# A new written-out order for a streamed sum of reciprocals: 30 row transfers, a ring of 41 rows, 72 sums of halves

## The chip, the core and the metric

The kernel runs on one core of a Trainium2 chip. The metric is the device time of one execution in microseconds (us). The core has five engines with queues of their own: TensorE (PE in the profile), VectorE (DVE), ScalarE (ACT), GpSimd (POOL) and SyncE (SP), which here only issues transfers. The profile shows a matmul's weight load as PEld.

## The reference

```python
x = abs(randn(32, 512, 1024)) as float32, + 1e-6
out = np.sum(1.0 / x, axis=-1)        # float32, shape (32, 512)
```

That is 16,384 sums of 1,024 reciprocals. The input is 67.11 MB and is read once; the output is 0.07 MB.

## The kernel before

**Tiling.** The 16,384 sums are laid out as 128 partitions by 128 "rows": row r of a partition is one vector of 1,024 numbers (4 KB), so a row over all partitions is 512 KB. Rows are loaded into `ring`, a buffer of R = 40 rows in SBUF; row r lies in place r mod R. A second SBUF buffer, `prod`, has NP = 22 slots of 512 numbers, and `ps` is the eight PSUM banks, 512 numbers each. `sums` collects one number per row.

**The arithmetic of a row.** A row is cut into halves a and b of 512 numbers. Because 1/a + 1/b = (a + b) / (ab), one reciprocal serves two elements. The reciprocal itself is exp(-ln(S ab)), with a scale S that the last step takes out again. So a row needs four steps, and the list below names each by a letter and the row number:

- the product ab, into a slot of `prod`: on POOL (`P`, line 199), or on DVE (line 220) with both halves from the ring (`W`), or with half b first copied into a PSUM bank by TensorE (`C`, line 209: a matmul with the identity) and then multiplied from there (`V`)
- `L`, the logarithm on ACT, in place in the slot (line 242)
- `E`, the exponential on ACT (line 251): in place, or, if the list gives `@bank`, into a PSUM bank
- `R`, the product with the numerator and the sum over the row, on DVE (line 267). There are two kinds. If TensorE has formed a + b in a PSUM bank (`S`, line 232: two matmuls with the identity that accumulate), `R` is 512 wide: slot times bank. If not, `R` is 1,024 wide: the row in the ring times the bank that holds the exponential, which is read twice.

One float32 matmul of the source appears as two MATMUL records in the profile, so an `S` is four records and a `C` two.

`D` loads rows (line 187). A number behind `+` takes several rows in one instruction (`L26+2` is rows 26 and 27). Numbers behind `@` give the slot for `L` and the bank for `C`, `S` and `E`. Rows 126 and 127 are loaded and worked in two halves each, called 126 to 129 in the list, with 256 numbers where others have 512.

**What sets the order.** There is no loop over rows: the string PLAN is the whole program, one token for each step, and each engine works through its own tokens in the order in which they stand. Before, rows 0 to about 80 follow a pattern of four rows: two with 1,024-wide `R` and an exponential in PSUM, two with `S`; ACT works mostly on pairs; about every eighth row is a `C` and `V`. From row 80 on the list is irregular. `note` (line 135) records which spaces each step reads and writes and drops waits that follow from others. The loads wait until the rows that stood in their places of the ring are done. The sums of rows 0 to 113 are written out in six transfers (line 289) when all of these are complete, the last 14 at the very end (line 291).

The tail of the list decides the end. Before, it reads:

```
R121 ... W124 ... R122 ... W125 S125@1 ... R123 P126 ... P127 ... S127@0 R124 ... P128 ... S128@2 ...
P129 R125 ... S129@3 ... R126 ... R127 ... R128 R129
```

Of the kernel before, what the change touches and what calls it, by code (L numbers as in the profile page):

```python
# [11 lines left out]
def kernel(  # L12
# [5 lines left out]
    nc = tc.nc  # L18
# [2 lines left out]
    D = 1024  # L21
    H = D // 2
    F = 128
    R = 40
    NP = 22
    LAST = F - 2  # L26
    DONE = 114
    S = float(2**17)

    PLAN = """
        D2 D10 D14 D14 P0+2 C3@3 S2@0 V3 P2 L0+2@0 C11@3 S3@1 E0+2@6 P4+2 V11 L2+2@2 R0 S6@2
        E2+2 R1 P6+2 L4+2@4 R2 R3 E4+2@6 S7@0 P8+2 L6+2@8 R4 S10@1 E6+2 R5 P10 L8+2@10 R6 R7  # L40
        S11@2 E8+2@6 L10+2@6 R8 E10+2 R9 D11 R10 R11 P12+2 C19@3 S14@0 V19 P14+2 L12+2@12
        S15@1 E12+2@6 S18@2 R12 P16+2 L14+2@16 R13 E14+2 R14 P18 L16+2@18 R15 S19@0 E16+2@6
        P20+2 L18+2@14 R16 S22@1 E18+2 R17 D9 P22+2 L20+2@20 R18 R19 E20+2@6 S23@2 P24+2
        L22+2@0 R20 E22+2 R21 L24+2@2 R22 R23 E24+2@6 P26 C27@3 R24 S26@0 P28+2 V27 R25 D7
        L26+2@4 C35@3 E26+2 S27@1 P30+2 V35 L28+2@8 R26 S30@2 R27 E28+2@6 P32+2 L30+2@10 R28
        S31@0 E30+2 R29 P34 L32+2@12 S34@1 R30 R31 E32+2@6 P36+2 S35@0 L34+2@6 R32 E34+2 R33
        D7 P38+2 S38@2 L36+2@16 R34 R35 E36+2@6 S39@1 P40+2 L38+2@18 R36 C43@3 E38+2 R37 D6
        S42@0 P42 L40+2@14 V43 R38 E40+2@6 P44+2 R39 S43@2 L42+2@20 R40 E42+2 S46@1 R41 D3
        P46+2 L44+2@0 R42 R43 E44+2@6 S47@0 P48+2 L46+2@2 R44 S50@2 E46+2 R45 P50 L48+2@4
        R46 C51@3 R47 E48+2@6 S51@1 P52+2 V51 R48 D6 L50+2@8 C59@3 E50+2 R49 P54+2 S54@0  # L50
        L52+2@10 V59 R50 E52+2@6 R51 S55@2 P56+2 L54+2@12 R52 E54+2 S58@1 R53 D5 P58
        L56+2@16 R54 R55 E56+2@6 S59@0 P60+2 L58+2@6 R56 S62@2 E58+2 R57 D4 P62+2 L60+2@14
        R58 R59 E60+2@6 S63@1 P64+2 L62+2@18 R60 S66@0 E62+2 R61 D4 P66 L64+2@20 R62 C67@3
        R63 E64+2@6 P68+2 S67@2 V67 R64 L66+2@0 S70@1 R65 D4 E66+2 P70+2 L68+2@2 R66 R67
        S71@0 E68+2@6 P72+2 L70+2@4 R68 D3 E70+2 R69 D2 C75@3 P74 L72+2@10 S74@2 R70 V75
        P76+2 E72+2@6 R71 S75@1 L74+2@8 R72 D2 E74+2 R73 D2 P80 S78@0 L76+2@12 R74 P81
        L80@16 R75 S79@2 E76+2@6 P78+2 L81@17 R76 D2 S81@1 E80@5 E81 R80 L78+2@6 W82 E78+2
        R81 R77 D1 D1 D1 D1 D1 P88 C85@6 S85@1 R78 P83 L88@18 V85 E88@7 R79 P84 S84@0
        L82+2@14 R88 E82+2@5 P86+2 L84+2@19 R82 D1 E84+2 R83 D1 D1 D1 C90@7 P91 L86+2@0
        S91@2 R85 P93 V90 E86+2@5 R84 P92 S90@1 L90+2@2 R87 L93@21 W89 L92@10 R86 D1 D1 D1  # L60
        D1 E93@7 P94 S97@0 E92@6 R93 E90+2 P97 S94@3 L89@11 R92 E89@7 P95 L97@8 R91 S95@4
        E97 R90 L94+2@4 W96 R97 P101 C99@6 L96@9 R89 E94+2 S100@0 P98 V99 E96@5 L101@12 R95
        P100 S99@1 L98@13 R96 E101@7 L99+2@16 R101 E98@6 P104 C103@5 R94 E99+2 S105@2 R98
        P102 L104@18 V103 E104@7 W105 L102+2@6 R100 P107+2 C106@6 L105@14 R104 E102+2@4
        S108@0 V106 E105 R102 L106+3@19 P109 S107@3 R103 P110 E106+3 R105 S106@4 R99 P111+2
        L109+2@0 R107 S112@1 R108 E109+2@6 R106 L111+2@10 P114 R109 S111@0 E111+2 R110 P113
        L114@15 R111 C115@7 P116 L113@2 R112 E114@6 V115 E113@5 S117@0 P117 R114 L116@3
        L115@8 P118 E116@7 R113 S118@1 E115@6 P119 L117+2@12 R116 E117+2 R115 P120 S120@2
        L119@9 R117 P121 L120@4 S121@3 R118 E119@7 E120 R119 P122 L121@5 S122@0 E121 R120
        P123 L122@18 R121 E122 W124 L123@6 R122 L124@7 W125 S125@1 E123@7 E124@6 R123 P126  # L70
        L125@14 P127 L126@16 S127@0 R124 E125 P128 L127@17 S128@2 E126@7 P129 R125 E127
        S129@3 L128@19 R126 L129@20 E128 R127 E129 R128 R129
    """.split()

    Ln = mybir.ActivationFunctionType.Ln
# [26 lines left out]
    make_identity(nc, ident)  # L102

    def parse(tok):
        body, _, b = tok[1:].partition("@")
        r, _, n = body.partition("+")
        return tok[0], int(r), int(n or 1), int(b) if b else None

    ops = [parse(tok) for tok in PLAN]

    pslot = {r + j: b + j for op, r, n, b in ops if op == "L" for j in range(n)}

    def place(r):
        if r < LAST:
# [9 lines left out]
    left = set(range(DONE))  # L124
    bank, copied, halves, summed = {}, {}, set(), set()

    history = {}
    begun = {}
    count = {}

    def note(engine, inst, reads=(), writes=()):
        inst = inst.ins
        known = dict(begun.get(engine, {}))
        before = {}
        for spaces, writing in ((reads, False), (writes, True)):
            for space in spaces:  # L140
                for other in history.get(space, ()):
                    if writing or other[3]:
                        before[other[0].name] = other
        needed = sorted(before.values(), key=lambda o: -o[4])
        for other in needed:
            o_inst, o_engine, o_tick, _, _, o_known = other
            if o_engine == engine:
                continue
            if o_tick <= known.get(o_engine, 0):
                tc.declare_no_dep(inst, o_inst, reason="implied by other waits")  # L150
                continue
            for e, t in o_known.items():
                known[e] = max(known.get(e, 0), t)
            known[o_engine] = max(known.get(o_engine, 0), o_tick)
        count[engine] = count.get(engine, 0) + 1
        begun[engine] = known
        entry = (engine, count[engine])
        if engine == "SP":
            entry = (f"load {count[engine]}", 1)
        for spaces, writing in ((reads, False), (writes, True)):  # L160
            for space in spaces:
                history.setdefault(space, []).append(
                    (inst, *entry, writing, sum(count.values()), known)
                )

    def rows(r, n, h=None):
        spaces = []
# [7 lines left out]
    def slots(r, n):  # L175
        return [("slot", pslot[q]) for q in range(r, r + n)]

    with tc.manual_schedule():
        for op, r, n, b in ops:
            p = pslot.get(r)  # L180
            if op == "D":
                n, r = r, loaded
# [45 lines left out]
            elif op == "S":  # L228
                bank[r] = b
                halves.add(r)  # L230
                for h in range(2):
                    inst = nc.tensor.matmul(  # L232
                        ps[:, b, : place(r)[2]],
                        lhsT=ident,
                        rhs=xs(r, h),
                        start=h == 0,
                        stop=h == 1,
                    )
                    note("PE", inst, rows(r, 1, h), [("bank", b)])
            elif op == "L":  # L240
                pg = prod[:, p : p + n, : place(r)[2]]
                inst = nc.scalar.activation(out=pg, in_=pg, func=Ln, scale=S)  # L242
# [1 line left out]
            elif op == "E":  # L244
# [5 lines left out]
                        bank[r + j] = b + j  # L250
                inst = nc.scalar.activation(out=rc, in_=pg, func=Exp, scale=-1.0)  # L251
                if b is None:
                    note("ACT", inst, writes=slots(r, n))
                else:
                    banks = [("bank", b + j) for j in range(n)]
                    note("ACT", inst, slots(r, n), banks)
            elif op == "R":
                q, at, w = place(r)
                other = ps[:, bank[r], :w]
                if r in halves:  # L260
                    row = prod[:, p, :w]
                else:
                    row = ring[:, q % R, at : at + 2 * w]
                    row = row.rearrange("p (h e) -> p h e", h=2)
                    other = other.unsqueeze(1).to_broadcast([P, 2, w])
                total = sums[:, q : q + 1]
                inst = nc.vector.tensor_tensor_reduce(  # L267
                    out=row,
                    in0=row,
                    in1=other,  # L270
                    scale=S,
                    scalar=total if q in summed else 0.0,
                    op0=mult,
                    op1=add,
                    accum_out=total,
                )
                summed.add(q)
                note(
                    "DVE",
                    inst,  # L280
                    [("bank", bank[r])],
                    slots(r, 1) if r in halves else rows(r, 1),
                )

                left.discard(r)
                if not left:
                    for c in range(0, DONE, DONE // 6):
                        part = slice(c, min(c + DONE // 6, DONE))
                        nc.sync.dma_start(out=out_v[:, part], in_=sums[:, part])
                    left.add(-1)  # L290
        nc.sync.dma_start(out=out_v[:, DONE:], in_=sums[:, DONE:])


# [28 lines left out]
```

## Time and profile before

| what | us |
|---|---|
| median of 3 executions (168.05 to 168.22) | 168.14 |
| span of the profiled execution, first to last instruction | 166.31 |
| median less span: what lies around the span | 1.83 |
| first product starts (row 0) | 5.66 |
| first work of TensorE and DVE (row 3) | 17.81, 19.89 |
| last DVE step ends, last transfer is issued | 164.0, 164.06 |
| busy: PE / DVE / ACT / POOL | 132.5 / 128.3 / 132.3 / 128.2 |
| share of 16 DMA engines in row transfers | 95.6% of the span |

The profile gives the span of its execution and no other time for it; the median is of other executions of the same program. The profile's times run from the start of the span. A busy PE is modelled, since matmuls are pipelined: the time from one record's start to the next is the better measure of its rate. The same holds for DVE and ACT, where an instruction overlaps the next by some 0.08 us. "Idle before" of a group of instructions is the time in which the engine stood still ahead of them, with what ended it.

### The profile page before, as it was taken

To read this page: it belongs to the slowest core of one execution; us is meant where nothing else is said; L and a number is where in the kernel's file an instruction comes from. 1 tells how busy PE (TensorE), PEld (TensorE's weight loads), DVE (VectorE), ACT (ScalarE), POOL (GpSimd) and SP (SyncE) were. 2 spreads that over 40 slices of the span, in tenths; PEclk is the share of its full clock that TensorE was granted. 3 is DMA by queue.
4 is the path that set the end of the run, shared out by engine and by line. 5 is a ranking of instruction groups with operands and counts; after the bars stand their busy time and mean duration, and the time that the engine had idled before them with its cause. 6 is when DMAs were issued, how large, how long until landed. Compare 5 with 4: busy or idle time off the path is not lost.

```text
span 166.3 us, 1348 instructions
## 1 busy us (share of the span) xinstructions
PE 132.5 (80%) x292; PEld 55.2 (33%) x292; DVE 128.3 (77%) x282; ACT 132.3 (80%) x157; POOL 128.2 (77%) x81
## 2 busy tenths in 40 slices
PE   0000799978855999999999999988699979989982
PEld 0000333333312444444343433324234424433351
DVE  0000119885787699898998898989899999999994
ACT  3040073949995899999799999996999999999992
POOL 1500795069995999999999999948977869999860
PEclk9999999999996999999999999999999999999999
DMA  5999999999998989999999999999999999999940
GB/s 189 536 394 394 441 441 441 441 441 441 441 441 349 509 368 446 430 417 438 441 434 434 406 426 446 429 424 424 414 437 437 414 410 428 410 409 410 400 139 4
DMA packets 5768, 67.26 MB, mean 404 GB/s; under 512 B 1536, under 2 KB 1536, under 8 KB 3200
## 3 DMA queue, kind: packets, MB, share of 16 engines
q1 hardware_dynamic: 5760, 67.18, 95.6%
q8 instruction: 2, 0.03, 0.1%
q14 instruction: 6, 0.05, 0.1%
HBM read 67.11 MB, written 0.07 MB: 404 GB/s over the span
## 4 chain that ended last, share of the span: by engine, by line
DMA 57%; PE 18%; ACT 8%; DVE 6%; POOL 6%; issue 3%; SPq 1%; ACTq 0%; POOLq 0%; DVEq 0%
DMA ring<-in_x_dram 57%; PE ps L232 15%; POOL prod L199 6%; ACT prod L242 4%; PE ps L209 3%; ACT ps L251 2%; DVE ring L267 2%; DVE prod L267 2%; ACT prod L251 2%; DVE prod L220 1%; SPq L187 1%; DVE sums L267 0%; ACTq L242 0%; POOLq L199 0%; DVEq L317 0%
## 5 line engine op out<-in xcount | busy, mean ns | idle before, releaser
L199 POOL TENSOR_TENSOR prod<-ring 128x1024 f32<-128x1024 f32 (+2 forms) x75 | 127.5, 1727 | 33.5 <-DMA ring<-in_x_dram 27.1
L232 PE MATMUL ps<-ring,ident 128*128 128x512 f32 (+1 forms) x260 | 116.9, 596 | 5.2 <-DVE sums L267 4.5
L242 ACT ACTIVATE prod<-prod 128x1024 f32<-128x1024 f32 (+2 forms) x78 | 68.5, 892 | 24.9 <-DVE prod L220 14.3
L267 DVE CUSTOM_DVE_ANT_1 ring<-ring,ps 128x1024 f32<-128x1024 f32 (+1 forms) x65 | 76.4, 1208 | 8.9 <-ACT ps L251 8.7
L232 PEld LDWEIGHTS ps<-ring,ident 128*128 128x128 f32 x260 | 49.2, 193 | 71.7 <-issue 51.6
L267 DVE CUSTOM_DVE_ANT_0 prod<-prod,ps 128x512 f32<-128x512 f32 (+1 forms) x63 | 40.9, 677 | 0.4 <-PE ps L232 0.4
L209 PE MATMUL ps<-ring,ident 128*128 128x512 f32 x32 | 19.3, 689 | 25.7 <-DMA ring<-in_x_dram 24.0
L251 ACT ACTIVATE ps<-prod 128x1024 f32<-128x1024 f32 (+2 forms) x41 | 34.1, 838 | 4.5 <-DVE sums L267 3.7
L251 ACT ACTIVATE prod<-prod 128x1024 f32<-128x1024 f32 (+3 forms) x37 | 34.4, 931 | 0.9
L220 DVE TENSOR_TENSOR prod<-ring,ps 128x512 f32<-128x512 f32 x16 | 10.9, 684 | 26.3 <-PE ps L209 26.3
L209 PEld LDWEIGHTS ps<-ring,ident 128*128 128x128 f32 x32 | 6.0, 213 | 36.0 <-issue 21.4
L267 DVE DVE_READ_ACCUMULATOR2_ANT sums<- 128x1 f32 x130 | 10.7, 82 | 0.0
L220 DVE TENSOR_TENSOR prod<-ring 128x512 f32<-128x512 f32 x6 | 4.1, 688 | 0.1
L84 ACT ACT_TABLE_LOAD x1 | 1.3, 1283 | 0.7 <-PEq L306 0.7
L267 DVE CUSTOM_DVE_ANT_0 prod<-prod,ps,sums 128x256 f32<-128x256 f32 x2 | 0.9, 475 | 0.0
masks.py:197 POOL MEMSET ident<- 128x128 f32 x1 | 0.2, 204 | 0.3 <-POOLq L306 0.3
masks.py:199 POOL TENSOR_SCALAR_AFFINE_SELECT ident<-ident 128x128 f32<-128x128 f32 x1 | 0.3, 292 | 0.1
L306 POOL MEMSET const-float32-0.0<- 128x1 f32 x1 | 0.1, 98 | 0.2 <-issue 0.2
L306 POOL MEMSET const-bfloat16-1.0<- 128x1 bf16 x1 | 0.1, 101 | 0.0
L306 POOL MEMSET const-uint8-127<- 128x1 uint8 x1 | 0.1, 101 | 0.0
L306 POOL MEMSET const-float32-1.0<- 128x1 f32 x1 | 0.1, 98 | 0.0
## 6 DMA issues: line engine op xcount, KB each, us to landing
ring<-in_x_dram SPq DMA_DIRECT2D x2, 7168.0 KB, 41.2
ring<-in_x_dram SPq DMA_DIRECT2D x2, 3584.0 KB, 29.3
ring<-in_x_dram SPq DMA_DIRECT2D x2, 3072.0 KB, 31.9
ring<-in_x_dram SPq DMA_DIRECT2D x3, 2048.0 KB, 34.0
ring<-in_x_dram SPq DMA_DIRECT2D x1, 5632.0 KB, 30.3
ring<-in_x_dram SPq DMA_DIRECT2D x5, 1024.0 KB, 31.8
ring<-in_x_dram SPq DMA_DIRECT2D x1, 5120.0 KB, 16.5
ring<-in_x_dram SPq DMA_DIRECT2D x1, 4608.0 KB, 30.7
```

The source lines that it names most:

```text
L84: nc.scalar.add_instruction(mybir.InstLoadActFuncSet(name=nc.get_next_instruction_name(), act_func_set_id=act_sets.index("natural_log_exp_ ...
L187: inst = nc.sync.dma_start(out=ring[:, a : a + m, at : at + 2 * w], in_=x_v[:, q : q + m, at : at + 2 * w],)
L199: inst = nc.gpsimd.tensor_tensor(out=prod[:, p : p + m, :w], in0=ring[:, a : a + m, at : at + w], in1=ring[:, a : a + m, at + w : at + 2 * w],
L209: inst = nc.tensor.matmul(ps[:, b, : place(r)[2]], lhsT=ident, rhs=xs(r, 1), start=True, stop=True,)
L220: inst = nc.vector.tensor_tensor(out=prod[:, p, :w], in0=xs(r, 0), in1=in1, op=mult)
L232: inst = nc.tensor.matmul(ps[:, b, : place(r)[2]], lhsT=ident, rhs=xs(r, h), start=h == 0, stop=h == 1,)
L242: inst = nc.scalar.activation(out=pg, in_=pg, func=Ln, scale=S)
L251: inst = nc.scalar.activation(out=rc, in_=pg, func=Exp, scale=-1.0)
L267: inst = nc.vector.tensor_tensor_reduce(out=row, in0=row, in1=other, scale=S, scalar=total if q in summed else 0.0, op0=mult, op1=add, acc ...
L306: nc = _bacc.Bacc("TRN2", target_bir_lowering=False, num_devices=1)
```

## The change

PLAN is replaced as a whole; R goes from 40 to 41 and NP from 22 to 20 (the two buffers together keep their size). Counted over the lists:

| | before | after |
|---|---|---|
| loads `D` (rows in each) | 33 (2, 10, 14, 14, 11, 9, 7, 7, 6, 3, 6, 5, 4, 4, 4, 3, 2 x4, then single rows) | 30 (14, 15, 12, 9, 9, 8, 8, 7, 6, 6, 5, 4, 4, 3, 2 x4, then single rows) |
| sums of halves `S` | 65 | 72 |
| copies `C` | 16 | 20 |
| DVE products `V` + `W` | 16 + 6 | 20 + 13 |
| POOL instructions (products) | 75 (108) | 77 (97) |
| ACT instructions `L` + `E` | 156 | 192 |
| `E` of one row, of two | 27, 50 | 91, 15 |

The rows with `W` are now 1, 7, 17, 14, 34, 40, 55, 62, 67, 82, 93, 124 and 125; before they were 82, 89, 96, 105, 124 and 125. `L` takes up to four rows in one instruction, and `L` and `E` of different rows alternate.

Two things are new in the code. A token can end in `!`: such an `E` (29 of them) waits, besides its own data, for the sum `S` of its rows, so that the `R` behind it has one engine less to wait for. And `note` now also drops a wait of an engine on itself where another wait implies it, and counts `sums` as a space that `R` writes. Two further letters, `A` and `Z`, can be parsed but do not occur in the list.

```diff
-    R = 40
-    NP = 22
+    R = 41
+    NP = 20
...
     PLAN = """
-        D2 D10 D14 D14 P0+2 C3@3 S2@0 V3 P2 L0+2@0 C11@3 S3@1 E0+2@6 P4+2 V11 L2+2@2 R0 S6@2
...
+        D14 D15 D12 W1 C3@0 W7 C5@1 V3 P0 C12@2 V5 P4 L0+2@0 S1@0 V12 E0@1 P6 L3+2@3 R0 S2@7
+        P10+2 L5+2@5 E3 S3@1 E1! L7@2 R1 P8+2 E5@2 S9@3 R3 E4@0 E6 R5 E7@1 P2 S6@4 L8+4@7 R7 P13
+        R4 S8@2 D9 L2@0 L12@11 R6 E2! L13@1 S11@0 R2 E10@1 E8+2! R10 S13@4 E11+2 R9 R8 E13 R11
+        S12@3 R13 W17 C18@0 W14 L17@0 C19@1 R12 P15+2 L14@1 V18 C26@2 E14@3 V19 L18@4 S15@0 R14
+        E18 P22 L15+2@2 V26 S18@1 E17@7 P20+2 E15! R17 E16@2 S21@3 L26@9 R15 R16 D9 P23+2
+        L19+2@5 S24@0 R18 E19+2@4 L21+2@7 R19 P27+2 S23@1 E21! R20 E22@2 S26@4 R21 P25 L27@10
+        L28@11 E26+3 S27@3 L23+3@12 R26 W34 C29@7 R27 P30 E24! C32@6 V29 E23! E25@3 R24 S30@4
...
+        R115 P120 L119@2 R116 E117 E119@2 P121 S121@4 R117 L120@0 E118! R119 P122 E120@0 S122@1
+        L121@1 R118 P123 L122@2 R120 E121! S123@2 E122 W124 L123@0 R121 L124@3 W125 E123 S125@0
+        R122 E124@3 P126 L125@4 R123 P127 L126@1 R124 S126@1 E125 P128 E126 S128@2 P129 L127@2
+        R125 L128@0 E127@3 R126 S129@4 L129@3 R127 E128 E129 R128 R129
...
-    def note(engine, inst, reads=(), writes=()):
+    def note(engine, inst, reads=(), writes=(), after=()):
...
+        for other in after:
+            before[other[0].name] = other
+            tc.add_manual_dep(inst, other[0].name, sync, reason="sums are ready")
...
-            if o_engine == engine:
-                continue
             if o_tick <= known.get(o_engine, 0):
                 tc.declare_no_dep(inst, o_inst, reason="implied by other waits")
                 continue
+            if o_engine == engine:
+                continue
...
-                    note("PE", inst, rows(r, 1, h), [("bank", b)])
+                    sum_of[r] = note("PE", inst, rows(r, 1, h), [("bank", b)])
...
-                    note("ACT", inst, writes=slots(r, n))
+                    after = [sum_of[r + j] for j in range(n) if held]
+                    note("ACT", inst, writes=slots(r, n), after=after)
...
-                    slots(r, 1) if r in halves else rows(r, 1),
+                    (slots(r, 1) if r in halves else rows(r, 1)) + [("sum", q)],
```

More of the change, by code (lines that the diff above doesn't have):

```diff
@@ L38 @@
     PLAN = """
-        D2 D10 D14 D14 P0+2 C3@3 S2@0 V3 P2 L0+2@0 C11@3 S3@1 E0+2@6 P4+2 V11 L2+2@2 R0 S6@2
[L40 to L72, printed above, removed]
+        D14 D15 D12 W1 C3@0 W7 C5@1 V3 P0 C12@2 V5 P4 L0+2@0 S1@0 V12 E0@1 P6 L3+2@3 R0 S2@7
+        P10+2 L5+2@5 E3 S3@1 E1! L7@2 R1 P8+2 E5@2 S9@3 R3 E4@0 E6 R5 E7@1 P2 S6@4 L8+4@7 R7 P13
@@ new lines @@
+        R4 S8@2 D9 L2@0 L12@11 R6 E2! L13@1 S11@0 R2 E10@1 E8+2! R10 S13@4 E11+2 R9 R8 E13 R11
[3 more added lines that the diff above has]
+        L28@11 E26+3 S27@3 L23+3@12 R26 W34 C29@7 R27 P30 E24! C32@6 V29 E23! E25@3 R24 S30@4
+        P31 L29+2@4 R25 P33 E29@0 V32 S31@5 E30 R23 P37 L31+2@6 R22 D8 S35@1 E32@3 P35+2 R29
@@ new lines @@
+        E31! L37@4 S28@2 R32 E37 P38 L33+4@0 R31 S37@0 R28 P39 L38@7 E33@2 W40 S38@3 E34@5 R33
+        D8 L39@16 P41+2 E35! R34 C47@7 L40@17 E38! S40@2 R35 R37 P46 L41+2@18 R38 S41@0 E36@1
+        R30 P49 E39+3 R36 P44+2 S43@3 V47 E42@4 L49@1 R40 L47@2 R41 S39@2 D7 E47 R42 P48 S47@0
+        P43 L48@0 R39 E48+2 L43+4@8 S49@1 W55 R47 P50+2 C53@2 E43! R49 E44+2@4 R43 C52@0 V53
+        E46@1 S48@3 P58 V52 R45 L50+4@12 P54 S51@0 R48 R46 P56+2 L54@1 E51 S55@3 R44 D6 E50@2
+        E54@1 R50 E52@7 S53@4 E53 L55+4@3 R52 D6 S57@2 P64 R51 R53 E58@7 P59+2 R54 E55! S59@0
@@ new lines @@
+        E56@4 E57! R55 R58 S60@1 P61 L60@19 L59@18 R56 D5 E60 P63 S65@3 E59! R57 L64@1 R59 P65
+        L63@0 S66@0 E63+2@4 P66 L65@6 R63 L66@7 W62 E65+2! W67 C71@2 L61+2@2 R64 P72+2 S67@4
+        L67@0 V71 E61@5 R66 E62@6 S70@2 R61 D4 P68 E67 R62 D4 P74 L68@1 S71@0 E68@5 R65 P70
+        L72+3@10 R60 S73@3 R67 P69 L70+2@8 R68 D3 S72@1 E73 L69@7 R73 P78 E70! E71+2 R70 C80@7
+        P75+2 E74@2 S81@3 R71 E69@4 V80 R69 D2 D2 P79 L75+2@4 S77@0 R72 E76@4 P77 R74 D2 E75@1
+        S80@5 P81 R75 L77+4@0 R76 D2 D1 P85 C84@1 L81@4 E77! C87@2 V84 P83 E78+2@6 R77 S83@4 V87
@@ new lines @@
+        E80! P86 L84@7 R78 D1 L83@8 S86@0 E84@1 W82 E83! R84 L82@0 S85@6 E81! R83 E82@2 R81
+        L85+2@5 R82 P88+2 C91@1 E85+2! S89@4 V91 R85 L91@4 R86 P90 L87+2@9 S92@6 R80 E91@0 P92
+        E87+2@1 R91 S90@3 L89+2@11 W93 R87 E89+2 P95+2 C94@5 L92+2@0 R88 S94@0 E93@1 V94 E92!
+        P97+2 R93 S96@2 L94+3@2 R89 R92 E94! S97@1 R79 D1 D1 D1 D1 D1 D1 D1 D1 D1 D1 L97@5 P99
+        E95@4 E96! R94 S100@5 P100 L98+2@6 R95 E97! P101 R96 S98@0 L100@8 R97 E98+3 P102 R90
+        C104@1 P103 L101@0 R100 E101@2 R98 S99@3 P105 L102+2@1 V104 R101 L104@3 P106 S103@0 E103
@@ new lines @@
+        R99 E102@1 P107+2 L105+2@4 R102 C109@7 E104+2@5 R103 S109@4 V109 E106@3 P111 R104
+        L107+2@18 S110@7 L109@6 P110 R106 E108@5 R105 P112+2 S113@0 L110+2@7 E107@1 R108 E109+2!
+        S112@2 R107 L112+2@0 P114+2 R109 E111@3 S115@6 E112+2 R110 R111 L114@2 P116 C117@1
+        L115@3 R113 E114@7 P118 S118@3 V117 L116@4 R112 E115! E116@0 P119 R114 S117@1 L117+2@5
+        R115 P120 L119@2 R116 E117 E119@2 P121 S121@4 R117 L120@0 E118! R119 P122 E120@0 S122@1
+        L121@1 R118 P123 L122@2 R120 E121! S123@2 E122 W124 L123@0 R121 L124@3 W125 E123 S125@0
@@ L104, in parse @@
     def parse(tok):
-        body, _, b = tok[1:].partition("@")
+        body, _, b = tok[1:].rstrip("!").partition("@")
         r, _, n = body.partition("+")
-        return tok[0], int(r), int(n or 1), int(b) if b else None
+        return tok[0], int(r), int(n or 1), int(b) if b else None, tok[-1] == "!"
     ops = [parse(tok) for tok in PLAN]
-    pslot = {r + j: b + j for op, r, n, b in ops if op == "L" for j in range(n)}
+    pslot = {r + j: b + j for op, r, n, b, _ in ops if op == "L" for j in range(n)}
     def place(r):
@@ L132 @@
     begun = {}
+    sum_of = {}
+    sync = mybir.DependencyInfo(
+        mybir.DependencyClass.Sync, mybir.DependencyReason.DATA
+    )
     count = {}
-    def note(engine, inst, reads=(), writes=()):
+    def note(engine, inst, reads=(), writes=(), after=()):
         inst = inst.ins
@@ L159, in note @@
             entry = (f"load {count[engine]}", 1)
+        last = None
         for spaces, writing in ((reads, False), (writes, True)):
             for space in spaces:
-                history.setdefault(space, []).append(
-                    (inst, *entry, writing, sum(count.values()), known)
-                )
+                last = (inst, *entry, writing, sum(count.values()), known)
+                history.setdefault(space, []).append(last)
+        return last
     def rows(r, n, h=None):
@@ L178 @@
     with tc.manual_schedule():
-        for op, r, n, b in ops:
+        for op, r, n, b, held in ops:
             p = pslot.get(r)
@@ L256 @@
                     note("ACT", inst, slots(r, n), banks)
+            elif op == "A":
+                q, at, w = place(r)
+                row = ring[:, q % R, at : at + 2 * w]
+                inst = nc.scalar.activation(out=row, in_=row, func=Ln)
+                note("ACT", inst, writes=rows(r, 1))
+            elif op == "Z":
+                q, at, w = place(r)
+                row = ring[:, q % R, at : at + 2 * w]
+                inst = nc.scalar.activation(
+                    out=row,
+                    in_=row,
+                    func=Exp,
+                    scale=-1.0,
+                    accum_out=sums[:, q : q + 1],
+                )
+                summed.add(q)
+                note("ACT", inst, writes=rows(r, 1) + [("sum", q)])
+                left.discard(r)
             elif op == "R":
@@ L281 @@
                     [("bank", bank[r])],
-                    slots(r, 1) if r in halves else rows(r, 1),
+                    (slots(r, 1) if r in halves else rows(r, 1)) + [("sum", q)],
                 )
                 left.discard(r)
[L286 to L290, printed above, removed]
+            if not left:
+                for c in range(0, DONE, DONE // 6):
+                    part = slice(c, min(c + DONE // 6, DONE))
+                    nc.sync.dma_start(out=out_v[:, part], in_=sums[:, part])
+                left.add(-1)
         nc.sync.dma_start(out=out_v[:, DONE:], in_=sums[:, DONE:])
```

## The prediction

> **What bounds the kernel now.** I read the page first, then stretches of the span, then the costs of single instructions, then the order of time at the start, around the products that DVE makes, and at the end.
>
> The page, with its slices and two of its DMA issues:
>
> ```profile
> span 166.3 us, 1348 instructions
> PE 132.5 (80%) x292; PEld 55.2 (33%) x292; DVE 128.3 (77%) x282; ACT 132.3 (80%) x157; POOL 128.2 (77%) x81
> ...
> DMA  5999999999998989999999999999999999999940
> GB/s 189 536 394 394 441 441 441 441 441 441 441 441 349 509 368 446 430 417 438 441 434 434 406 426 446 429 424 424 414 437 437 414 410 428 410 409 410 400 139 4
> ...
> q1 hardware_dynamic: 5760, 67.18, 95.6%
> ...
> ring<-in_x_dram SPq DMA_DIRECT2D x1, 5632.0 KB, 30.3
> ...
> ring<-in_x_dram SPq DMA_DIRECT2D x9, 512.0 KB, 13.8
> ```
>
> The DMA engines are full from the second slice to the 38th: the loads are the bound, and the engines follow. The 11 rows of 5632 KB move in some 13 us but land 30.3 us after their issue, so the queue never ran dry.
>
> Three stretches (busy time and count of each engine, TensorE's clock, DMA share, GB/s):
>
> ```profile
> 17.70:34.60 16.90, 15.55 (x28) 6.16 (x28) 10.34 (x21) 10.05 (x10) 9.44 (x5) 1.00 1.00 434
> 51.60:65.50 13.90, 13.89 (x29) 6.18 (x30) 11.29 (x23) 11.30 (x12) 13.81 (x7) 0.90 0.99 425
> 145.00:157.40 12.40, 11.88 (x27) 4.50 (x25) 12.30 (x28) 12.17 (x20) 12.28 (x10) 1.00 1.02 408
> ```
>
> Rows of 524 KB at 441 GB/s (slices with 14-row transfers) take 1.19 us, at 408 GB/s (single-row transfers, 145 to 157.4) 1.285 us: a transfer costs 0.1 us beyond its bytes.
>
> TensorE's first records:
>
> ```profile
> 17.81 2.04 PE L209 MATMUL ps<-ring,ident 128*128 128x512 f32 x2 [17.81 <-DMA ring<-in_x_dram]
> 19.65 3.62 PE L232 MATMUL ps<-ring,ident 128*128 128x512 f32 x4
> 23.06 1.36 PE L209 MATMUL ps<-ring,ident 128*128 128x512 f32 x2
> 24.26 1.02 PE L232 MATMUL ps<-ring,ident 128*128 128x512 f32 x2
> ```
>
> The chain of waits has 28 later records in 12.02 us, 0.43 us each; here the first eight take 6.45 us instead of 3.44. TensorE starts slow and loses 3.0 us.
>
> The products on DVE, by form, and one beside its neighbour on POOL:
>
> ```profile
> L220 DVE TENSOR_TENSOR prod<-ring,ps 128x512 f32<-128x512 f32 x16 | 10.9, 684 | 26.3 <-PE ps L209 26.3
> L220 DVE TENSOR_TENSOR prod<-ring 128x512 f32<-128x512 f32 x6 | 4.1, 688 | 0.1
> ...
> 128.03 0.69 DVE L220 TENSOR_TENSOR prod<-ring 128x512 f32<-128x512 f32 x1
> 128.71 1.28 POOL L199 TENSOR_TENSOR prod<-ring 128x512 f32<-128x512 f32 x1 [1.13 <-DMA ring<-in_x_dram]
> ```
>
> The sixteen `V` (one half from PSUM) run beside POOL's products, 53.72 within 51.69 to 55.29 for one. The six `W` (both halves from the ring) stand at 111.51, 122.79, 128.03, 136.22, 157.37 and 158.69, and all fall into gaps of POOL; none overlaps a POOL product by more than 0.13 us. What happens when they meet is not in this trace.
>
> The end, on DVE and SP:
>
> ```profile
> 158.69 0.69 DVE L220 TENSOR_TENSOR prod<-ring 128x512 f32<-128x512 f32 x1
> ...
> 163.54 0.47 DVE L267 CUSTOM_DVE_ANT_0 prod<-prod,ps,sums 128x256 f32<-128x256 f32 x1
> 163.95 0.08 DVE L267 DVE_READ_ACCUMULATOR2_ANT sums<- 128x1 f32 x1
> 164.06 0.33 SPq L291 DMA_DIRECT2D out_dram<-sums  x1
> ```
>
> W125 starts 0.02 us after row 125 has landed (158.67 in the trace's landing records), and DVE works without a gap to 164.03: the end is that landing plus 5.34 us of DVE, plus 2.28 us of output. Span 166.31; the median lies 1.83 us above it, and I add that to every span below.
>
> **The change part by part.**
>
> *Loads.* Three transfers fewer: 3 x 0.1 = 0.3 us earlier at the end, so row 125 lands at 158.37. Do the loads still have their places free in time? Counting the work of TensorE and DVE ahead of each release, the tightest (rows 41 to 49, behind S8) is free near 36 and due at the DMA engines at 52.4, 16 us of lead; before, the shortest lead was 15 (issued at 35.1, first packet at 50.7). SP has nothing else queued behind these. Hidden; if it were not, each us late would be one us of time.
>
> *Start.* The first landing is 14 rows instead of 2. Rows 0 to 11 were there at 17.7; two rows more and a transfer less give 20.05. The work of rows 0 and 1 done by 10.2 moves behind it.
>
> *TensorE.* Records: 69 `S` x 4 + 20 `C` x 2 = 316 of 0.43 us, and 12 half-wide of 0.21: 138.2 us (before: 280 and 12, 122.9). From 20.05, with 3.0 us of slow start: 161.25 if it never waits. The last sum, S129, is needed where R129 starts, near 163.2. So TensorE has 2.0 us of room in 143; before it had about 18. Its work is also cut to the landings: from that of row 121 (153.2) on, 9.4 us are left, to 162.6, which leaves 0.6.
>
> *DVE.* Start to start, 1.14 for a 1,024-wide `R`, 0.61 for a 512-wide one, 0.605 for a product: before 64, 63 and 22 of them, 126.2 us with three small ones; after 57, 70 and 33, 129.1. From 20.05 that ends at 149.2: 14 us to spare, most of it spent waiting for `S`.
>
> *ACT.* Start to start 0.52 for one row, 0.96 for a pair, 1.07 where the exponential follows its own logarithm. Before: 46 singles, 100 pairs at a mean of 1.02, 2 triples, 8 half-wide: 131.8. After: 134 x 0.52 + 38 x 0.96 + 6 triples x 1.41 + 6 quads x 1.85 (estimates on the same slope) + 8 x 0.31 = 128.3. Room of 14 us; splitting pairs costs 0.04 us a row, and alternating gains 0.11 a pair. An `E` with `!` blocks the `L` and `E` behind it until TensorE has the sum; `R` needed that sum anyway. Price between -1.1 us of DVE (22 waits fewer at 0.05) and some us of ACT within its room; on the path I take 0.
>
> *POOL.* 97 products for 108: 115 us for 127. Room.
>
> *The tail.* From W125: 0.62 + 3 x 0.61 (R122, R123, R125) + 1.14 (R124) + 0.36 (R126) + 0.61 (R127) + 0.40 + 0.49 = 5.42, against 5.34. With the landing: 164.03 - 0.3 + 0.08 = 163.81, span 166.1, time 167.9. That is the sum if nothing new waits.
>
> *The thirteen `W`.* Seven stand from W17 to W67, and in the list most stand at a landing ahead of POOL's next product: W17 and W14 ahead of P15+2, W34 ahead of P30, W55 ahead of P50+2, W67 ahead of P72+2. That works only if DVE is there when the rows land. For the first I walk it. TensorE does 3 `C` and 8 `S` up to S13: 3 x 0.86 + 8 x 1.72 + 3.0 = 19.3, so 39.4. R13 needs S13 and runs 39.6 to 40.2. Then comes W17, but rows 14 to 28 land at 38.2 and POOL has P15+2 from then to 40.6, and P22, P20+2, P23+2, P27+2, P25 behind it without a gap. Without the slow start, DVE would have been waiting at 37.2. So they meet. If one blocks the other, W17 starts at 40.6; S15 needs the bank that V18 frees, and V18 stands behind W17, W14 and R12. DVE first both times: V18 ends at 43.5, when TensorE is due at S15 (43.7), cost 0. One POOL product (1.24) between the two: 1.1 us of TensorE. POOL first each time: 3.5. I take 1.1, the case between. W34 comes the same way (TensorE ends S26, ahead of it, at 54.0; its row lands at 52.6): half a single product, 0.6. W40, W55 and W67 sit before pairs of 2.33; an even chance of half of one, 0.6 each. From there on DVE's lateness passes to TensorE through the banks: by counts, releases such as R59 for S66 or R65 for S73 come only 0.2 to 0.3 us before TensorE wants them. I pass on 0.4 of each 0.6. Sum: 1.1 + 4 x 0.4 = 2.7, less the room of 2.0: 0.7 us. Ends: 0 (they do not hinder each other, or DVE goes first), and one whole POOL instruction in front of every W, about 6 us of TensorE, 4 beyond the room.
>
> By the Trainium skill, "SBUF — State Buffer", "Who interferes with whom", a DVE instruction with two SBUF inputs and a GpSimd instruction that reads SBUF exclude each other, and whichever came first keeps the other out for its whole length; one SBUF input does not contend. The gaps around the six `W` and the overlaps of the `V` agree, but no `W` here tried to start inside a POOL product. By this rule the term is 0.7 or more; without it the time would be 167.9.
>
> **Sum.** 167.9 + 0.7 = 168.6.
>
> **The rivals.**
>
> 1. *The list holds.* DVE wins the meetings, or they cost TensorE less than 2.0 us in all: the mechanism decides from there. For it: DVE has 14 us to spare. Against it: TensorE's room. 167.9, between 167.5 and 168.4.
> 2. *The last rows land earlier still.* In the landing records the slowest DMA engine ends 0.3 us behind the middle one at 51.5, and 1.8 behind from 112 on; packets of the queues q8 and q14, which fetch instructions, hit single engines, 0.35 to 0.65 us each, and nothing evens it out. If the new program's hits spread over other engines, W125 starts up to 0.5 us earlier: 167.4. A further hit on the same one would give 168.4.
> 3. *POOL always goes first.* 3.5 us at W17 and W14, more at each later one: 172 and up.
>
> **How the numbers follow.** Within 0.2% (0.34 us) is about what this measurement cannot tell from no change: 167.80 to 168.48. TensorE is held up beyond its room (forecast): 0.52, of it 0.08 for rival 3, and a few of its cases (0.05) end below 168.48. The list holds: 0.34, of it 0.22 within the bound and 0.12 faster. Landing earlier: 0.14, faster but for 0.01. So faster 0.25, the same 0.28, slower 0.47. The range reaches from 167.4 (rival 2) to 172 (one POOL instruction ahead of each W); the forecast's own is 168.3 to 170.5.
>
> **What would show it.** First landing near 20.05, rows 0 to 28 near 38.2. W17 starting where a POOL product ends, about 40.6; TensorE then idle before S15 with DVE as its releaser. TensorE at 95% or more of the time from 20 to 161, and DVE waiting for it at 512-wide `R`. The DMA queue again full to the end, with row 125 at 158.4. Wrong would be: W beside POOL at full speed, or TensorE idle for under 2 us before row 70. Then the time is 167.9.

## The result, and the profile after

The changed kernel takes 174.76 us (median; 174.68 to 175.77), against 168.09 in the runs beside it: 1.0408 times the time before, with a 95% interval of 1.0378 to 1.0438. It is slower, which was forecast, but by 6.7 us where 0.5 was forecast, and outside the range that ended at 172. Ratios here are of fast executions alone: one of the kernel before (171.61) and one of the run with two rows first (175.83) ran in a slower state. They can lie a little off the ratio of two medians. The profiled execution of the changed kernel took 175.77, 1.0 above its median; the clock records of its trace have TensorE at a granted clock of 0.5 from 103.10 to 106.51 us, and its mean granted clock was 0.99, where that of the other three (174.68 to 174.78) was 1.0.

The page after, its first lines, the DMA slices and the shares of the chain that ended last; below it the same shares before:

```profile
span 173.9 us, 1422 instructions
PE 144.6 (83%) x328; PEld 62.2 (36%) x328; DVE 140.5 (81%) x293; ACT 133.4 (77%) x193; POOL 121.4 (70%) x83
...
DMA  6999999999989999999999999999999999998000
...
DVE 38%; PE 33%; DMA 11%; ACT 11%; issue 4%; DVEq 0%; ACTq 0%
```

```profile
DMA 57%; PE 18%; ACT 8%; DVE 6%; POOL 6%; issue 3%; SPq 1%; ACTq 0%; POOLq 0%; DVEq 0%
```

The loads are as dense as before but end in the 37th slice of a longer span: the last slices are empty. The DMA share of the last chain is 11%; it was 57%. DVE's is 38% and was 6%, TensorE's 33% and was 18%. DVE's busy time rose from 128.3 to 140.5 us where the instruction count asked for about 3 more. POOL does 11 products less and is busy 121.4 us, not the 115 of the count.

The products, by form (busy, mean ns of one, idle time before):

```profile
L195 POOL TENSOR_TENSOR prod<-ring 128x512 f32<-128x512 f32 x53 | 70.0, 1343 | 35.3 <-DMA ring<-in_x_dram 21.2 <-ACT ps L247 12.5 <-DVE sums L282 1.3
L195 POOL TENSOR_TENSOR prod<-ring 128x1024 f32<-128x1024 f32 x20 | 48.7, 2448 | 10.0 <-ACT prod L247 6.4 <-ACT ps L247 3.2 <-DMA ring<-in_x_dram 0.3
L216 DVE TENSOR_TENSOR prod<-ring 128x512 f32<-128x512 f32 x13 | 18.8, 1464 | 20.7 <-DMA ring<-in_x_dram 20.7
L216 DVE TENSOR_TENSOR prod<-ring,ps 128x512 f32<-128x512 f32 x20 | 13.4, 680 | 1.9 <-PE ps L205 1.7
```

The twenty `V` take 680 ns, as before (684). The thirteen `W` take 1464 ns; the six of before took 688. That is 13 x 0.776 = 10.1 us more on DVE. Ten of them are longer than 0.69: W7 1.75, W17 1.75, W14 1.76, W34 1.31, W40 0.98, W55 2.34, W62 1.45, W67 1.76, W82 2.05, W93 1.82. Where a `W` is long, the POOL product that starts during it is long too: 1.71 to 1.74 us for one row instead of 1.28, 2.82 to 2.84 for two instead of 2.37.

W17 and W14, on DVE, POOL and TensorE in turn (merged lines: a total and a count):

```profile
40.08 3.43 DVE L216 TENSOR_TENSOR prod<-ring 128x512 f32<-128x512 f32 x2
...
38.93 6.82 POOL L195 TENSOR_TENSOR prod<-ring 128x1024 f32<-128x1024 f32 x3 [6.40 <-ACT prod L247]
...
44.78 1.55 PE L228 MATMUL ps<-ring,ident 128*128 128x512 f32 x3 [1.25 <-DVE prod L216]
```

One by one: P15+2 runs from 38.93 to 41.29. W17 starts at 40.08 and ends at 41.83. P22 starts at 41.25 and takes 1.72, to 42.97. W14 starts at 41.76 and ends at 43.52. P20+2 starts at 42.93 and takes 2.82. A `W` that takes longer than 0.69 us is called a meeting below. The engines take turns: a `W` waits for the rest of the product that is running on POOL, and the next product on POOL waits until that `W` is through. TensorE then stands idle for 1.25 us before S15, until DVE has freed its bank.

DVE's last stretches (PE, PEld, DVE, ACT, POOL busy, TensorE's clock, DMA share, GB/s):

```profile
105.00:125.00 20.00, 19.78 (x45) 8.47 (x44) 17.84 (x39) 16.14 (x24) 15.05 (x11) 0.96 0.99 423
125.00:145.00 20.00, 18.79 (x43) 7.73 (x43) 19.43 (x43) 18.71 (x24) 16.16 (x11) 1.00 1.00 423
145.00:157.40 12.40, 12.33 (x29) 5.11 (x28) 12.40 (x28) 12.37 (x19) 11.10 (x8) 1.00 1.02 407
```

and its end:

```profile
164.78 0.69 DVE L216 TENSOR_TENSOR prod<-ring 128x512 f32<-128x512 f32 x1
...
166.00 0.69 DVE L216 TENSOR_TENSOR prod<-ring 128x512 f32<-128x512 f32 x1
...
171.32 0.08 DVE L282 DVE_READ_ACCUMULATOR2_ANT sums<- 128x1 f32 x1
171.43 0.33 SPq L305 DMA_DIRECT2D out_dram<-sums  x1
```

W124 starts at 164.78. Its row landed at 157.72, so DVE is 7.1 us behind the loads; before, it was 0.03 behind (157.37 against 157.34). From W125 on it needs 5.40 us, against 5.34. The 7 us of lateness are most of the loss of this execution (175.77 less 168.14).

How the lateness gets there is in the chain that ended last, from W62 and W67 on:

```profile
97.52 3.06 DVE prod L216 x2
...
102.37 8.83 PE ps L228 x16
...
112.06 5.15 PE ps L228 x12
```

It runs over the two meetings on DVE, then to 118.08 over TensorE, which from 97 to 105 us had been busy for only 5.96 us of 8 (7.83 in the run with one factor from PSUM below), and from there for the most part over DVE with W82 and W93. So both engines carry it. The 8.83 us hold the stretch at half the clock: in the run with the marks without effect, where the clock was 1.0, the same 16 records take 7.20.

### The profile page after: what moved, and what is told of

It is laid out like the page before. It is cut to its first block, busy times and chain, and to the rows that moved or that the text cites. A ratio compares the mean times of both kernels' runs of the same rounds, so it can differ in the third digit from the quotient of the medians.

```text
span 173.9 us, 1422 instructions
## 1 busy us (share of the span) xinstructions
PE 144.6 (83%) x328; PEld 62.2 (36%) x328; DVE 140.5 (81%) x293; ACT 133.4 (77%) x193; POOL 121.4 (70%) x83
## 4 chain that ended last, share of the span: by engine, by line
DVE 38%; PE 33%; DMA 11%; ACT 11%; issue 4%; DVEq 0%; ACTq 0%
PE ps L228 28%; DVE ring L282 16%; DMA ring<-in_x_dram 11%; DVE prod L216 11%; DVE prod L282 10%; ACT prod L238 6%; PE ps L205 5%; ACT prod L247 3%; ACT ps L247 2%; DVE sums L282 1%; DVEq L331 0%; DVEq L216 0%; ACTq L238 0%; ACTq L247 0%
## 5 line engine op out<-in xcount | busy, mean ns | idle before, releaser
L195 POOL TENSOR_TENSOR prod<-ring 128x512 f32<-128x512 f32 (+2 forms) x77 | 120.7, 1604 | 47.5 <-DMA ring<-in_x_dram 21.6
L228 PE MATMUL ps<-ring,ident 128*128 128x512 f32 (+1 forms) x288 | 126.7, 594 | 4.6 <-DVE prod L216 3.3
L238 ACT ACTIVATE prod<-prod 128x512 f32<-128x512 f32 (+4 forms) x83 | 68.5, 848 | 29.8 <-POOL prod L195 20.8
L228 PEld LDWEIGHTS ps<-ring,ident 128*128 128x128 f32 x288 | 54.1, 192 | 75.7 <-issue 54.8
L282 DVE CUSTOM_DVE_ANT_1 ring<-ring,ps 128x1024 f32<-128x1024 f32 (+1 forms) x58 | 68.6, 1205 | 1.9 <-ACT ps L247 1.8
L282 DVE CUSTOM_DVE_ANT_0 prod<-prod,ps 128x512 f32<-128x512 f32 x70 | 45.6, 677 | 6.5 <-ACT prod L247 5.1
L247 ACT ACTIVATE prod<-prod 128x512 f32<-128x512 f32 (+3 forms) x57 | 40.1, 718 | 0.9 <-PE ps L228 0.5
L247 ACT ACTIVATE ps<-prod 128x512 f32<-128x512 f32 (+2 forms) x52 | 32.3, 632 | 5.9 <-DVE sums L282 3.8
L216 DVE TENSOR_TENSOR prod<-ring 128x512 f32<-128x512 f32 x13 | 18.8, 1464 | 20.7 <-DMA ring<-in_x_dram 20.7
L205 PEld LDWEIGHTS ps<-ring,ident 128*128 128x128 f32 x40 | 8.1, 210 | 31.8 <-issue 28.8
L216 DVE TENSOR_TENSOR prod<-ring,ps 128x512 f32<-128x512 f32 x20 | 13.4, 680 | 1.9 <-PE ps L205 1.7
```

Of the source, the lines that this page charges most:

```text
L195: inst = nc.gpsimd.tensor_tensor(out=prod[:, p : p + m, :w], in0=ring[:, a : a + m, at : at + w], in1=ring[:, a : a + m, at + w : at + 2 * w],
L205: inst = nc.tensor.matmul(ps[:, b, : place(r)[2]], lhsT=ident, rhs=xs(r, 1), start=True, stop=True,)
L216: inst = nc.vector.tensor_tensor(out=prod[:, p, :w], in0=xs(r, 0), in1=in1, op=mult)
L228: inst = nc.tensor.matmul(ps[:, b, : place(r)[2]], lhsT=ident, rhs=xs(r, h), start=h == 0, stop=h == 1,)
L282: inst = nc.vector.tensor_tensor_reduce(out=row, in0=row, in1=other, scale=S, scalar=total if q in summed else 0.0, op0=mult, op1=add, acc ...
```

## The experiments

Theory 1: a DVE product with both factors in the ring and a POOL product exclude each other; the ten meetings cost DVE 10 us, and DVE is then late at the end. Rivals: TensorE has no room for 138 us of matmuls (2), the first landing comes too late (3), ACT is held up by the new waits (4), and, of the forecast, TensorE's slow start makes DVE miss the gaps.

Four kernels in one series; the kernel before took 168.25 us there. The changed kernel did not run again: gains are counted from its 174.76, and the kernel before, which ran in every series, took between 168.09 and 168.25.

**One factor from PSUM.** Nine `W` read their second factor from the bank that DVE had just used:

```diff
+                other = op == "W" and 7 < r < 124
                 in1 = xs(r, 1) if op == "W" else ps[:, copied[r], :w]
+                if other:
+                    in1 = ps[:, seen[-1], :w]
...
```

> The changed kernel, but the nine products W17, W14, W34, W40, W55, W62, W67, W82 and W93 take their second factor from the PSUM bank that DVE read just before, instead of from the ring; list, order and instruction counts stay. The result of these rows is not the reference's, since the factor is another row's. Theory 1 (a DVE product with both factors in the ring and a POOL product exclude each other, which lengthens 10 of 13 W by 10.1 us in all and makes DVE the bound): the nine take 0.69 us instead of 0.98 to 2.35, POOL's lengthened products (1.72 and 2.83) go back to 1.28 and 2.37, and the time falls by 6 to 7.5 us, to 167.3 to 168.8. Theory 2 (TensorE has 138 us of matmuls and no room, and DVE only follows it): banks are held 0.6 us longer, nothing is gained, 174 to 176. Theory 3 (the first landing at 20.7 instead of 5.6 is what cannot be made up): less than 1 us gained.

Measured: 169.1 us (168.71 to 169.75), 1.0052 of before (1.0030 to 1.0073): 5.7 us gained. Its products by form:

```profile
L196 POOL TENSOR_TENSOR prod<-ring 128x512 f32<-128x512 f32 x53 | 67.7, 1303 | 28.5 <-DMA ring<-in_x_dram 26.0 <-ACT ps L254 1.9 <-DVE sums L290 0.2
L196 POOL TENSOR_TENSOR prod<-ring 128x1024 f32<-128x1024 f32 x20 | 47.4, 2382 | 14.0 <-DMA ring<-in_x_dram 12.5 <-ACT prod L245 1.3
L220 DVE TENSOR_TENSOR prod<-ring,ps 128x512 f32<-128x512 f32 x29 | 19.6, 684 | 2.7 <-PE ps L206 1.5 <-ACT ps L254 1.0
L220 DVE TENSOR_TENSOR prod<-ring 128x512 f32<-128x512 f32 x4 | 3.7, 955 | 20.7 <-DMA ring<-in_x_dram 20.7
```

Same instructions, same places in the list, one operand elsewhere: 684 ns, and POOL's products are back at their length. Only W7 among the four left is long (1.75). W124 starts at 157.91, 0.1 us after its row. This settles theory 1 for the larger part of the loss, and against theories 2 and 3 as its cause: TensorE has as many matmuls and the first rows land as late (20.71 us). The 5.7 fall short of the 6 to 7.5 expected, and 0.85 us against the kernel before remain.

**TensorE warm.** Eighteen matmuls of the identity into bank 0 ahead of the list:

```diff
+        for _ in range(18):
+            inst = nc.tensor.matmul(
+                ps[:, 0, :],
+                lhsT=ident,
+                rhs=ident.unsqueeze(1).to_broadcast([P, 4, P]),
...
+            note("PE", inst, (), [("bank", 0)])
```

> The changed kernel with 18 matmuls of the identity into bank 0 ahead of the list, so that TensorE is busy from about 1.5 to 20 us and no longer slow when the first rows land. Nothing else changes. If TensorE's slow start is the root (it makes DVE late, and so W late at the landings): W17, W34 and W55 come before POOL's product, most W take 0.69, 168 to 169.5. Theory 1 as the after trace shows it (W7, with DVE in time, waited 1.06 us for P0, which started between W1 and W7; so the engines take turns): 3 us gained at the start for TensorE, but W14 still waits for P15+2 and the later ones meet POOL as before; 172 to 174.5. Theory 2 (TensorE's room): 3 us gained, 171.5 to 172.

Measured: 175.4 us (174.7 to 175.65), 1.0423 of before (1.0394 to 1.0451): nothing gained, and above the 172 to 174.5 of theory 1 too. At like clock there is no difference from the changed kernel either: 174.7 for the one execution at a granted clock of 0.998, 175.17 to 175.65 for the three at 0.99. The first six records of TensorE took 2.84 us instead of 4.69, so it was warm, and DVE was in time for W17: on DVE and POOL,

```profile
38.76 3.46 DVE L225 TENSOR_TENSOR prod<-ring 128x512 f32<-128x512 f32 x2 [0.26 <-DMA ring<-in_x_dram]
...
38.80 4.54 POOL L204 TENSOR_TENSOR prod<-ring 128x1024 f32<-128x1024 f32 x2 [6.39 <-DMA ring<-in_x_dram]
```

W17 takes 0.69, P15+2 waits for it and takes 2.86, and W14, next on DVE, waits for the whole of P15+2 and takes 2.85. Being first once does not help a pair of `W`. The slow start is not the root: with it gone, nine `W` still meet POOL's products, and the time is the same.

**Two rows first.** `D14` at the head becomes `D2 D12`:

```diff
-        D14 D15 D12 W1 C3@0 W7
+        D2 D12 D15 D12 W1 C3@0 W7
```

> The changed kernel with the first transfer of 14 rows cut into 2 and 12 rows, so that rows 0 and 1 are there at 5.6 us; the rest of the list is the same. Theory 3 (late start): 2 us or more gained. Theory 1: W1, P0 and the logarithm behind them go ahead, so W7 no longer meets P0 (1.06 us of DVE), one transfer more costs 0.1 us at the end: between 1.2 us gained and nothing.

Measured: 172.14, 172.54 and 174.58 us (a fourth execution 175.83), 1.0292 of before (1.0211 to 1.0373). The mean of the three is 1.7 us below the changed kernel, between the 1.2 that theory 1 allowed and the 2 that theory 3 asked for, and with a spread of 2.4 us it decides nothing between them. In the profiled execution (172.54) there are fewer meetings: W7 takes 0.69, and so does W82, which now comes ahead of P88+2; the 13 `W` take 1217 ns in the mean instead of 1464, together 3.2 us less.

**Nine products on POOL.** `W17` becomes `P17`, and so on:

```diff
-        S12@3 R13 W17 C18@0 W14 L17@0
+        S12@3 R13 P17 C18@0 P14 L17@0
```

> The changed kernel with the same nine products moved from DVE to POOL, at their places in the list (P17 for W17 and so on). Theory 1: DVE loses 9 x 0.605 us of work and the 9.0 us by which these were lengthened; POOL goes from 121 to about 128 us busy, less 5 us of waiting for DVE; 167.3 to 168.8 unless a product on POOL then comes late. Theory 2: TensorE is the bound, 174 to 175. The result is the reference's.

Measured: 168.83 us (168.37 to 169.19), 1.0039 of before (1.0027 to 1.0051): 5.9 us gained. POOL is busy 128.6 us and hides it:

```profile
L195 POOL TENSOR_TENSOR prod<-ring 128x512 f32<-128x512 f32 x62 | 78.7, 1295 | 29.2 <-DMA ring<-in_x_dram 26.7 <-ACT ps L247 1.5 <-DVE sums L282 0.7
L216 DVE TENSOR_TENSOR prod<-ring 128x512 f32<-128x512 f32 x4 | 3.7, 954 | 20.8 <-DMA ring<-in_x_dram 20.8
```

A second series (before: 168.23 us) asks where the loss arises, whether it can be made in the old list, and about the new waits.

**The same in the kernel before.** Seven `V` become `W`, and their copies `C` go:

```diff
-        L0+2@0 C11@3 S3@1 ... P26 C27@3 R24 S26@0 P28+2 V27 R25
+        L0+2@0 C11@3 S3@1 ... P26 R24 S26@0 P28+2 W27 R25
```

> The kernel before, with seven of its V (rows 27, 35, 43, 51, 59, 67 and 75) turned into W: both factors from the ring, and the seven copies C on TensorE left out. Nothing else changes; the result is the reference's. Theory 1: a W costs DVE the rest of the POOL product that runs when it starts (POOL is 95% busy there), so the seven take 1.2 to 1.8 us in place of 0.68, and POOL's products behind them 1.72 or 2.83; DVE gets 4 to 8 us more work, POOL 3 us, TensorE 6 us less; time 168.2 to 172, by how much of it DVE's and POOL's waits absorb. Rival (W is slow only because the new list crowds them with late engines): they take 0.69, and the time is the same or less.

Measured: 175.91 us (175.85 to 176.21), 1.0464 of before (1.0449 to 1.0480). It is more than the 172 at most that was expected:

```profile
L219 DVE TENSOR_TENSOR prod<-ring 128x512 f32<-128x512 f32 x13 | 21.8, 1678 | 0.0
L219 DVE TENSOR_TENSOR prod<-ring,ps 128x512 f32<-128x512 f32 x9 | 6.1, 681 | 24.3 <-PE ps L208 24.3
...
53.27 2.65 DVE L219 TENSOR_TENSOR prod<-ring 128x512 f32<-128x512 f32 x1
```

The list and the loads of before, TensorE relieved of seven copies, and the loss is there. It is larger than the seven: the four `W` of rows 82 to 105, which had each fallen into a gap of POOL and taken 0.69, now take 2.53, 1.24, 1.55 and 1.01, because DVE comes at other times. Once late, a `W` meets POOL, and that makes DVE later.

**The marks without effect.**

```diff
-                    after = [sum_of[r + j] for j in range(n) if held]
+                    after = [sum_of[r + j] for j in range(n) if False]
```

> The changed kernel with the marks ! without effect: the 29 exponentials no longer wait for the sum, and the R behind them waits for ACT and TensorE both. Theory 1: the marks are not the cause; DVE gets some 20 waits of 0.05 us back; 174.5 to 176. Theory 4 (ACT, held by TensorE, makes everything late): 1 us or more gained, 170 to 173.5.

Measured: 174.57 us (174.44 to 175.58), 1.0394 of before (1.0364 to 1.0425). No different from the changed kernel; theory 4 falls.

**Only the early four, only the late five**, with one factor from PSUM as in the first run (the late five have `50 < r < 124`):

```diff
-                other = op == "W" and 7 < r < 124
+                other = op == "W" and 7 < r < 50
```

> As the run with one SBUF input, but for W17, W14, W34 and W40 alone (lengthened by 3.0 us together in the changed kernel); the other W stay. If the time lost early is made up in DVE's waits for TensorE: 0 to 1.5 us gained, 173.3 to 174.8. If each lost us is carried to the end: 3 us gained, near 171.8. The result of these rows is not the reference's.

> As the run with one SBUF input, but for W55, W62, W67, W82 and W93 alone (lengthened by 6.0 us together). If what is lost early is made up: nearly the whole effect, 4.5 to 6 us gained, 169 to 170.3. If the early ones carry to the end: 171 to 171.8. The result of these rows is not the reference's.

Measured: the early four 175.0 us (174.52 to 175.52), 1.0407 of before (1.0381 to 1.0433), the late five 170.02 (169.99 to 170.12), 1.0113 (1.0096 to 1.0129). With only the early four changed nothing is gained at the end. The trace shows where the gain goes: W62 starts at 96.20 instead of 97.44, but P72+2, which runs on POOL at that time, ends at 98.09 (98.34 in the changed kernel), so W62 takes 2.44 us instead of 1.45 and ends only 0.25 earlier. With the late five changed, 4.7 of the 5.7 us are gained; the remaining 0.9 are what the early four bring once the late five are out of the way. With the late five changed, W124 starts at

```profile
158.99 0.69 DVE L220 TENSOR_TENSOR prod<-ring 128x512 f32<-128x512 f32 x1
```

The start of W124, how far this is behind the landing of its row in the trace's landing records, and the time of the same, profiled, execution go together (before: span 166.31 and 1.83 around it):

| kernel | W124 starts, behind landing (us) | time of that execution (us) |
|---|---|---|
| before | 157.37, 0.03 | 168.14 |
| nine with one factor from PSUM | 157.91, 0.1 | 168.88 |
| late five with one factor from PSUM | 158.99, 1.4 | 170.0 |
| changed | 164.78, 7.1 | 175.77 |
| before, seven more `W` | 165.53, 7.8 | 176.21 |

**What is left.** The two runs without the nine meetings are still 0.6 to 0.9 us slower than before. A third series (before: 168.19 us) puts the nine products on POOL, cuts the first transfer into two, and in the second kernel warms TensorE too; the edits are those shown above, together.

> The changed kernel with the nine products on POOL and, besides, the first transfer cut into 2 and 12 rows. The first 2-row transfer also starts the DMA engines earlier on (40 rows had landed at 51.3 on the middle engine before, 41 rows at 52.8 after, 0.4 later than 1.2 us a row gives). If that start is what still separates the run with the products on POOL from the kernel before (0.6 us): 168.2 to 168.5. If it is TensorE's room: no change, 168.6 to 169.

> The same, with 18 matmuls of the identity ahead, so that TensorE does not start slow. If TensorE's room is what still separates the two: 3 us more of it, and the end goes back to the landing of row 125 plus 5.4 us: 167.8 to 168.3. If not: as the run without them.

Measured: 168.5 us (168.24 to 168.85), 1.0019 of before (1.0010 to 1.0028); and with TensorE warm 168.43 (168.17 to 168.88), 1.0012 (1.0003 to 1.0021). The two cannot be told apart. This excludes less than it seems: in the profiled execution with the 18 matmuls TensorE's granted clock was 0.5 from 21.29 to 24.71 us, and its first six records took 4.54 us, against 5.46 without the matmuls, so it gained 0.9 us at the start and not 1.9. And room at the start is not room at the end. In the run with one factor from PSUM the chain that ended last is

```profile
138.87 15.07 DMA ring<-in_x_dram
...
153.99 8.04 PE ps L235 x20
```

and then 2.5 us of DVE: behind the landing of row 121 (153.95) it is TensorE's sums that end last. Both kernels of the third series have the same 8.04 us, from 153.58 and 154.05. In the kernel before the chain stays with the loads to 157.34 and holds only 1.72 us of TensorE behind them. That these sums are the rest of the difference is likely, and was not tested. Against the nine on POOL alone, the early two rows bring 0.3 us. No version ran faster than the kernel before.

## Why the prediction was wrong in size, point by point

- *The mechanism* was named and is right: `W` and POOL's products exclude each other, `V` does not contend. The rule of the Trainium skill ("SBUF — State Buffer", "Who interferes with whom") agrees: 688 ns without a meeting, 1464 in the mean here, and 684 again with one SBUF input. Among waiting instructions the engines take turns in these traces. One reading was not exact: W124 did start inside a POOL product before the change, 0.13 us ahead of its end, and took 0.69 all the same.
- *The walk to W17* held, in part by luck. Forecast: R13 to 40.2, W17 then, TensorE idle 1.1 us before S15. Measured: W17 starts at 40.08, 1.25 us idle with DVE's product as releaser. The case between was the right one. But the first landing came 0.6 us late, and TensorE's slow start lost 2.0 us (six records in 4.53, start to start, where 0.43 each makes 2.58) and not 3.0; the two errors cancel.
- *The meetings were miscounted.* Six `W` were priced, in five terms that add up to 3.5 us (1.1 for W17 and W14 together, 0.6 for each of four). These six lost 5.8 us: W34 and W40 cost 0.62 and 0.29, as priced or less, W55 and W67 1.65 and 1.07 where 0.6 stood, W17 and W14 1.06 and 1.07. Four more that were not priced, W7, W62, W82 and W93, lost 4.3. An even chance was too kind: W40, W55 and W67 all met a product, and POOL is busy for 70% of the span.
- *The failing step is "I pass on 0.4 of each 0.6 ... less the room of 2.0".* I let the loss reach the end only through TensorE, and took DVE's 14 us to spare as cover. Measured, 4.7 of the late five's 6.0 us reach the end, 0.8 of each us, with no room taken off; the early four's 3.0 us, which I had let count in the same way, cost 0.9 us without the late five and nothing beside them. The spare time lies early: DVE stands still for 4.9 us from 20 to 38.2, 3.3 from there to 105, 2.2 from 105 to 125, 0.6 from 125 to 145 and not at all from 145 to 157.4. A loss at W82 or W93 has little of it left. The loss at W62 and W67 goes over TensorE as well, as I had it, but whole: these two `W` are 1.8 us longer, and TensorE is busy 1.9 us less between 97 and 105 than in the run with one factor from PSUM. The term of 0.7 measures 5.7.
- *The loads* were sized wrong. Row 125 was to land 0.3 us earlier (158.37); it landed at 159.01, 0.34 later than before. The slope of 0.1 us for a transfer does not show in the end: over the runs here row 125 lands between 158.57 (30 transfers) and 159.37 (31), with 33 transfers at 158.67 and 159.07. The first landing came at 20.67, not 20.05.
- *TensorE's room* at the start mattered less than I said: 1.9 us gained there changed nothing in the changed kernel, and 0.9 nothing in the one with the products on POOL. The 0.6 us of room behind the landing of row 121 is the closer figure: there TensorE ends last as soon as the meetings are gone.
- *ACT and the marks*: forecast 0 on the path, measured no difference. *POOL*: room, as forecast. *The tail*: 5.42 us forecast (its terms add up to 5.45), 5.40 measured.
- *The rivals.* "The list holds" put 167.9 to a kernel without the meetings; 168.4 to 169.1 is what such kernels take. "The last rows land earlier still" did not happen: the slowest DMA engine ends 1.85 us behind the middle one at row 125, where before it was 1.82. The one that reached past 172 assumed that POOL always goes first; the time came there for another reason, ten meetings in turns.

## What to carry to other kernels

Spare time of an engine is worth something only where it lies: sum an engine's work from each late point to the end, not over the span. And time gained ahead of a meeting can be lost in it, as W62 showed. Before moving an operation to another engine, look at what its operands share with work that is in flight: here the place of one operand of nine products (SBUF or PSUM) was worth 5.7 us, with list and order unchanged. Gaps that an instruction falls into in one trace are no property of the instruction; a small delay upstream closes them, as the four old `W` showed.

## What the runs showed of the hardware that was not expected

- A product on DVE with both factors in SBUF and products on POOL that follow each other without a gap alternate in all traces here: the DVE product waits for the rest of one POOL product, never for two (the longest took 2.87 us for 0.69), and the next POOL product is longer by 0.3 to 0.5 us.
- The 16 DMA engines end apart: the last one lands its part of row 125 1.4 to 2.0 us behind the middle one in these runs, more than any change in the number of transfers moved the landing. What sets the spread from run to run stays open.
- In some of the profiles TensorE's granted clock is 0.5 for stretches of 3.41 us. Executions of four kernels (changed; TensorE warm; marks without effect; early four) took 175.2 to 175.8 us where the mean granted clock was 0.99, and 174.4 to 174.8 where it was 0.998 or more. The kernel before, with such a stretch from 51.04 to 54.45 in its profile, shows no such difference: 168.05 to 168.5 us at a mean of 0.977 to 0.98, 167.96 to 168.72 at 0.998 or more. What brings a stretch on stays open.
